# The compression's w1 tiles in the pool of 4 KB tiles instead of the weights' stage buffers

## The chip, the cores and the metric

The kernel runs on one core of a Trainium2 chip. The metric is the device time of one execution in microseconds (us). The kernel before takes 1110.68 us, the median of three runs (1110.3 to 1111.24).

## What is computed

Two layers of a decoder trunk on 512 tokens of width 1024, all in float32. Each layer normalises x, projects it once into the inputs of four token mixers, runs the mixers, and merges them under gates:

```
h = rmsnorm(x, norm_g[l])
c = split_columns(h @ w_in[l])
y_a = dilated_window_attention(...) * silu(c["a_gate"])
y_b = mla_attention(...) * silu(c["b_gate"])
y_c = nsa_attention(...) * silu(c["c_gate"])
y_d = stick_breaking_attention(...) * silu(c["d_gate"])
for i, y in enumerate((y_a, y_b, y_c, y_d)):
    gate = sigmoid(h @ w_merge[l, i] + b_merge[l, i])
    merged = merged + gate * (y @ w_branch[l, i])
x = x + merged @ w_out[l]
```

Branch C first compresses its keys and values: overlapping blocks of 32 tokens (31 of them), each flattened to 2048 numbers, go through a small network, once for keys and once for values:

```
blocks = tok[:, idx] + pos_emb
hid = gelu(blocks.reshape(B, n_cmp, NSA_CMP_BLOCK * Dk) @ w1 + b1)
return hid @ w2 + b2
```

Here w1 is 2048 x 128 for keys and again for values: four tiles of 1024 x 128 (512 KB each) per layer.

## The kernel before

Every projection is done by TensorE (PE) in float32r with three passes: a weight tile is loaded by SyncE's DMA queue (SP) into a stage buffer, then split into a high and a low part (w5 tiles) by ACT and DVE (L175 and L176, five of eight or ten k-slices) and by POOL (L100 and L185, the rest); `proj_T` then issues 24 matmuls of 128x512 (L189, L190, L191 in turn) into a PSUM accumulator pd. There are 3 stage buffers, 4 w5 tiles, 3 pd accumulators, 2 score banks pss, and 11 buffers in the pool of 4 KB tiles (per partition) called s4, which holds q, k, v, gates and the merge's accumulators. A tile takes any buffer that is free; a load or a write into it waits until the former tile's last reader is done. A merge chunk is a projection of w_merge (24 matmuls) followed by six matmuls with the branch's result y.

The program is written in one sequence, but a scheduler orders the instructions of each engine by priority and by its own idea of when operands are ready; each engine then works strictly in that order. The scores (`qk_unit`, L290) of branch A go through DVE (minimum, L300), ACT (exp, L302), DVE (L303) and POOL (L305), are transposed on PE (L325), copied by ACT (L327) and multiplied with v (L331). Branch D, stick breaking, runs in pairs of heads: scores, mask (L738), min (L740), exp (L741), ln after a table load (L744), max (L746), a running sum (L751), a subtraction (L752), exp (L753), then transposes and L331. Both are interleaved with projections of other branches, which fill PE while the other engines work.

`compress` stands in the program behind the first merge chunks. It projects the columns c_kc and c_vc (pd_1978 in layer 0), adds the positions (L609), projects c_ks and c_kw (pd_2023), and multiplies by w1 (L629, 32 matmuls of 32x128 into pd_2068): each w1 tile was loaded (L626) into a stage buffer and is used as it comes, without a split. The accumulator is copied by ACT (L632), summed over four groups by PE (L635), and the small network follows on DVE (L636 to L657).

Of the kernel before, what the change touches and what calls it, by code (L numbers as in the profile page):

```python
# [16 lines left out]
P = 128  # L17
# [69 lines left out]
def hybrid_trunk(ctx: ExitStack, tc: tile.TileContext, x, norm_g, w_in, mla_q_norm, mla_w_uq, mla_kv_norm,  # L87
# [16 lines left out]
    def mk(pool, shape, dt, tag, bufs):  # L104
        n_names[0] += 1
        return pool.tile(list(shape), dt, tag=tag, name=f"{tag}_{n_names[0]}", bufs=bufs)

    def s4(shape, dt=F32):
        return mk(sb, shape, dt, "s4", N_S4)
# [22 lines left out]
    def stage(shape):  # L132
        return mk(wp, shape, F32, "stage", 3)
# [309 lines left out]
    for l in range(DEPTH):  # L443
# [140 lines left out]
        def compress():  # L584
# [37 lines left out]
            acc = ps_d()  # L622
            for s_ in range(2):
                for hf in range(2):
                    w1 = stage([P, 8, P])
                    nc.sync.dma_start(w1, nsa_w1[l, s_, 1024 * hf:1024 * hf + 1024].rearrange("(q p) c -> p q c", p=P))  # L626
                    for q in range(8 * hf, 8 * hf + 8):
                        g = 32 * (q % 4)
                        T.matmul(acc[g:g + 32, s_ * P:(s_ + 1) * P], blocks[s_][:, q], w1[:, q % 8], start=q < 4,  # L629
                                 stop=q >= 12, skip_group_check=True)  # L630
# [76 lines left out]
        merge_chunks(l, ((0, 1),), y, am, mT)  # L707
        gd = gate_chunks("d_gate")
        ks, kw, kc, vbd = compress()
        merge_chunks(l, ((1, 0),), y, am, mT)  # L710
        c_q = [q_chunk("c_q", c, cscale[:, c:c + 1]) for c in range(2)]
# [177 lines left out]
```

## Time and profile before

| | |
|---|---|
| Median of three runs | 1110.68 us |
| The profiled execution | 1114.14 us |
| Its span | 1112.4 us |
| PE matmul busy | 1078.8 us, 97% |
| PE weight loads busy | 861.7 us |
| DVE, ACT, POOL busy | 541.5, 441.2, 464.4 us |
| HBM read | 95.67 MB, 90 GB/s over the span with what is written |

The span is the time from the first to the last instruction of the profiled execution; its own time is 1.7 us longer. The ends of matmuls are modelled, so busy time of PE is an upper bound of its work; the distance between the starts of two matmuls tells more.

### The profile page before, as it was taken

Reading aid. Unit: us, or ns where it says so; the run is one execution under the profiler, and the core shown is the slowest. Engines: PE = TensorE matmul, PEld = TensorE weight load, DVE = VectorE, ACT = ScalarE, POOL = GpSimd, SP = SyncE. Lnnn points to the kernel's source line nnn. Section 1 sums busy time; section 2 is a strip of 40 time slices with the busy share of each in tenths; the row PEclk is TensorE's granted clock in tenths of the full one; section 3 lists DMA queues with packets and bytes.
Section 4 is the critical chain, followed back from the end, with each engine's and each line's share of the span. In section 5 each row is a group of like instructions: output and inputs, shape, how many; then the busy total and the mean of one; then the engine's idle time right before and its main releaser. Section 6 shows DMA issues by size and latency. Waiting matters only on the chain.

```text
span 1112.4 us, 15422 instructions
## 1 busy us (share of the span) xinstructions
PE 1078.8 (97%) x5652; PEld 861.7 (77%) x5652; DVE 541.5 (49%) x1008; ACT 441.2 (40%) x894; POOL 464.4 (42%) x506
## 2 busy tenths in 40 slices
PE   8999999979999999999999999999799999999997
PEld 5888787758678878787888887777577787878876
DVE  6435444485835344234453546445955544532342
ACT  5424444344434434223243344435453343432232
POOL 5243354333436466452011544324334464656421
PEclk9999999989999999999999999999899999999999
DMA  7422232522232221435413322225223222233322
GB/s 245 103 57 76 76 105 58 162 66 72 71 91 75 71 73 48 133 93 153 121 57 96 95 74 70 76 77 166 62 71 94 72 71 72 72 92 90 117 77 76
DMA packets 161677, 100.87 MB, mean 91 GB/s; under 512 B 14913, under 2 KB 151489, under 8 KB 161602
## 3 DMA queue, kind: packets, MB, share of 16 engines
q1 hardware_dynamic: 160880, 98.75, 30.9%
q10 hardware_dynamic: 722, 1.14, 0.3%
q8 instruction: 45, 0.74, 0.3%
q14 instruction: 30, 0.25, 0.1%
HBM read 95.67 MB, written 4.19 MB: 90 GB/s over the span
## 4 chain that ended last, share of the span: by engine, by line
PE 83%; DVE 7%; DMA 4%; ACT 2%; issue 2%; POOL 1%; SPq 0%; POOLq 0%; DVEq 0%; ACTq 0%
PE pd L191 22%; PE pd L189 22%; PE pd L190 22%; PE po L331 5%; PE pss L290 5%; PE pt L325 4%; DMA stage<-in_w_out_dram 4%; DVE x L751 2%; DVE w L176 1%; ACT y L175 1%; DVE x L746 1%; DMA x<-in_x_dram 1%; PE pd L629 0%; PE pt L678 0%; DVE x L752 0%
## 5 line engine op out<-in xcount | busy, mean ns | idle before, releaser
L191 PE MATMUL pd<-hT,w 128*128 128x512 f32 x832 | 333.2, 401 | 11.2 <-DVE w L176 11.2
L189 PE MATMUL pd<-hT,w 128*128 128x512 f32 x832 | 335.0, 403 | 7.8 <-ACT w L175 4.7
L190 PE MATMUL pd<-hT,w 128*128 128x512 f32 x832 | 334.2, 402 | 0.0
L100 POOL TENSOR_SCALAR w<-stage 128x640 fp32r<-128x640 f32 (+1 forms) x104 | 78.1, 751 | 297.8 <-PE pd L190 192.3
L191 PEld LDWEIGHTS pd<-hT,w 128*128 128x128 f32 x832 | 157.8, 190 | 48.4 <-DVE w L176 13.6
L189 PEld LDWEIGHTS pd<-hT,w 128*128 128x128 f32 x832 | 157.8, 190 | 44.5 <-ACT w L175 6.2
L176 DVE TENSOR_TENSOR w<-stage,w 128x640 fp32r<-128x640 f32 (+2 forms) x116 | 157.5, 1357 | 69.7 <-ACT w L175 57.1
L190 PEld LDWEIGHTS pd<-hT,w 128*128 128x128 f32 x832 | 157.8, 190 | 33.6 <-issue 0.7
L185 POOL TENSOR_TENSOR w<-stage,w 128x640 fp32r<-128x640 f32 (+1 forms) x104 | 161.7, 1555 | 49.7 <-PE pd L190 39.8
L175 ACT ACTIVATE w<-stage 128x640 fp32r<-128x640 f32 (+2 forms) x116 | 87.5, 759 | 105.9 <-PE pd L190 65.8
L302 ACT ACTIVATE su<-su,stat 128x128 f32<-128x128 f32 (+3 forms) x128 | 71.2, 557 | 76.4 <-DVE stat L300 75.9
L395 POOL TENSOR_TENSOR s<-s,th 128x512 f32<-128x512 f32 x48 | 77.9, 1623 | 31.7 <-DVE th L394 31.7
L327 ACT ACTIVATE pt<-pt 128x384 f32<-128x384 f32 (+2 forms) x120 | 57.6, 521 | 77.3 <-PE pt L325 77.1
L394 DVE SCALAR_TENSOR_TENSOR th<-th,pd 128x512 f32<-128x512 f32 x48 | 32.9, 686 | 110.5 <-PE pd L191 95.2
L387 ACT ACTIVATE th<-pd,bmT 128x512 f32<-128x512 f32 x64 | 43.9, 685 | 74.6 <-PE pd L191 74.5
L305 POOL TENSOR_SCALAR su<-su,stat 128x128 f32<-128x128 f32 (+3 forms) x64 | 36.7, 579 | 79.2 <-DVE stat L303 78.1
L325 PE MATMUL pt<-small,su 128*128 128x128 f32 x336 | 60.4, 280 | 0.0
L307 POOL TENSOR_SCALAR su<-su,stat,cg 128x128 f32<-128x128 f32 (+3 forms) x64 | 41.0, 647 | 43.1 <-DVE stat L303 42.9
L189 PE MATMUL pd<-y,w 128*128 128x512 f32 x128 | 51.0, 401 | 1.9 <-ACT th L387 1.7
L325 PEld LDWEIGHTS pt<-small,su 128*128 128x128 f32 x336 | 40.2, 140 | 15.6 <-issue 8.5
L191 PE MATMUL pd<-y,w 128*128 128x512 f32 x128 | 50.5, 394 | 0.0
L190 PE MATMUL pd<-y,w 128*128 128x512 f32 x128 | 50.5, 394 | 0.0
(239 smaller groups left out, 1582.5 us busy)
## 6 DMA issues: line engine op xcount, KB each, us to landing
stage<-in_w_merge_dram SPq DMA_DIRECT2D x64, 512.0 KB, 3.9
stage<-in_w_in_dram SPq DMA_DIRECT2D x38, 512.0 KB, 3.9
stage<-in_w_branch_dram SPq DMA_DIRECT2D x64, 128.0 KB, 3.8
stage<-in_w_out_dram SPq DMA_DIRECT2D x16, 512.0 KB, 3.9
stage<-in_w_in_dram SPq DMA_DIRECT2D x20, 256.0 KB, 3.2
stage<-in_nsa_w_dram SPq DMA_DIRECT2D x8, 512.0 KB, 4.0
stage<-in_w_in_dram SPq DMA_DIRECT2D x8, 352.0 KB, 4.6
x<-in_tab_a_dram SPq DMA_DIRECT2D x4, 512.0 KB, 4.2
```

Of the source, the lines that this page charges most:

```text
L100: G.tensor_scalar(o, i, 1.0, 1.0, op0=OP.mult, op1=OP.mult)
L175: A.activation(hi, src, AF.Copy)
L176: V.tensor_tensor(lo, src, hi.bitcast(F32), op=OP.subtract)
L185: G.tensor_tensor(lo[:, a:], src[:, a:], hi[:, a:].bitcast(F32), op=OP.subtract)
L189: T.matmul(acc, sh, mh, start=start, stop=False)
L190: T.matmul(acc, sh, ml, start=False, stop=False)
L191: T.matmul(acc, sl, mh, start=False, stop=stop)
L290: T.matmul(s[:, :width], q[:, qt * P:(qt + 1) * P], k[:, :width], start=i == 0, stop=i == len(passes) - 1)
L302: A.activation(e[:, :width], e[:, :width], AF.Exp, scale=-1.0, bias=st[:, 0:1], accum_out=st[:, 1:2])
L325: T.transpose(pt[:, i], u[0][h][:, kb * P:(kb + 1) * P], ident)
L327: ready = A.activation(pT[:, :n], pt[:, :n], AF.Copy)
L395: G.tensor_tensor(acc[:, j], acc[:, j], th, op=OP.add)
```

## The change

One call in `compress` takes its tile from the pool s4 instead of stage. The shape, the load and the matmuls stay. The pools keep their sizes (11 buffers in s4, 3 in stage).

```
             for s_ in range(2):
                 for hf in range(2):
-                    w1 = stage([P, 8, P])
+                    w1 = s4([P, 8, P])
                     nc.sync.dma_start(w1, nsa_w1[l, s_, 1024 * hf:1024 * hf + 1024].rearrange("(q p) c -> p q c", p=P))
```

The scheduler answers with another order on every engine from this point to some way into branch D; the same happens in layer 1. Three places of layer 0 show it. The names carry the numbers of the tiles; s_420 to s_423 (stage_2069 to stage_2099 before) are the four w1 tiles.

On PE, right after the projection of c_ks and c_kw (pd_2023), before the change: the w1 matmuls lie between the transposes (pt) and scores (pss) of branch A.

```order
L629 MATMUL pd_2068<-stage_2069,s_410_2011 32x128 x8
L629 MATMUL pd_2068<-stage_2079,s_410_2011 32x128
L325 MATMUL pt_1706<-small,su_1673 128x128
L629 MATMUL pd_2068<-stage_2079,s_410_2011 32x128
L325 MATMUL pt_1712<-small,su_1682 128x128
L629 MATMUL pd_2068<-stage_2079,s_410_2011 32x128 x2
L290 MATMUL pss_1724<-y_297_1524,y_292_1486 128x384 x2
L290 MATMUL pss_1733<-y_298_1528,y_292_1486 128x384 x2
```

And with the change, at the end of the stretch of branch A and of D's scores of pair 0 (s_152, s_157, s_158) that now follows pd_2023 directly: the w1 matmuls come behind the first two scores of D's pair 1, and the projection of merge chunk (1, 0), pd_2147, begins only after them.

```order
L290 MATMUL pss_2693<-s_168_937,s_163_899 128x512 x2
L290 MATMUL pss_2697<-s_169_941,s_163_899 128x512 x2
L629 MATMUL pd_2068<-s_420_2069,s_410_2011 32x128 x8
L189 MATMUL pd_2147<-hT_75,w_434_2141 128x512
L190 MATMUL pd_2147<-hT_76,w_434_2141 128x512
L191 MATMUL pd_2147<-hT_75,w_435_2142 128x512
```

Before, pd_2147 and the next chunk's pd_2191 lay between these scores; now all of D's scores of pair 0 come ahead of both.

On SP, the order of the loads from the compression on, before the change:

```order
L626 DMA stage_2069<-in_nsa_w_dram 128x8x128
L626 DMA stage_2079<-in_nsa_w_dram 128x8x128
L626 DMA stage_2089<-in_nsa_w_dram 128x8x128
L626 DMA stage_2099<-in_nsa_w_dram 128x8x128
L238 DMA stage_2138<-in_w_merge_dram 128x8x128
L238 DMA stage_2138<-in_w_branch_dram 128x2x128
L238 DMA stage_2182<-in_w_merge_dram 128x8x128
L238 DMA stage_2182<-in_w_branch_dram 128x2x128
L238 DMA stage_2227<-in_w_in_dram 128x8x128
```

And now, after stage_2138, stage_2182, stage_2227 and stage_2265:

```order
L238 DMA stage_2305<-in_w_merge_dram 128x8x128
L238 DMA stage_2305<-in_w_branch_dram 128x2x128
L626 DMA s_420_2069<-in_nsa_w_dram 128x8x128
L626 DMA s_421_2079<-in_nsa_w_dram 128x8x128
L626 DMA s_422_2089<-in_nsa_w_dram 128x8x128
L626 DMA s_423_2099<-in_nsa_w_dram 128x8x128
L829 DMA s_863_4487<-in_x_dram 128x512
```

The four w1 loads moved behind five weight tiles.

On DVE, in the stick-breaking chain of pair 0 (x_493 to x_497, su_2562, su_2565), before the change: the weight split w_448, which the projection pd_2226 needs, stands inside the chain.

```order
L746 TENSOR_TENSOR su_2565<-su_2562,su_2565 128x512
L644 TENSOR_SCALAR gelu_2116<-gelu_2116 128x64
L751 SCALAR_TENSOR_TENSOR x_497_2564<-x_497_2564 128x128 x2
L751 SCALAR_TENSOR_TENSOR x_497_2564<-x_497_2564 128x384 x2
L176 TENSOR_TENSOR w_448_2230<-stage_2227,w_447_2229 128x640
L392 SCALAR_TENSOR_TENSOR s_432_2137<-th_2216,pd_2218 128x512
```

And with the change it stands behind the whole chain and the first masks of pair 1:

```order
L752 TENSOR_TENSOR x_494_2561<-x_494_2561,x_497_2564 128x1024
L738 TENSOR_TENSOR x_521_2687<-pss_2693,mask_tab 128x512
L738 TENSOR_TENSOR x_521_2687<-pss_2697,mask_tab 128x512
L752 TENSOR_TENSOR su_2562<-su_2562,su_2565 128x512
L392 SCALAR_TENSOR_TENSOR s_432_2137<-th_2172,pd_2174 128x512
L636 TENSOR_SCALAR hid_2067<-pt_2111,b_401_1966 128x32
L176 TENSOR_TENSOR w_448_2230<-stage_2227,w_447_2229 128x640
```

The chain itself is the same; its place relative to the splits is not.

## Rows read from the trace of the kernel before

**Rows 1.** The page, busy time by engine, share of the span, and instructions.

```profile
PE 1078.8 (97%) x5652; PEld 861.7 (77%) x5652; DVE 541.5 (49%) x1008; ACT 441.2 (40%) x894; POOL 464.4 (42%) x506
```

**Rows 2.** Waits of PE: total us, times, longest us.

```profile
PE pd L191 <- DVE w L176: 11.2, 4, 4.8
```

**Rows 3.** Table of stretches, layer 0: busy PE, PEld, DVE, ACT, POOL; clock; DMA share, GB/s.

```profile
235.00:240.00 5.00, 1.64 (x5) 0.59 (x4) 4.97 (x5) 3.00 (x5) 4.75 (x3) 0.85 0.00 0
240.00:245.00 5.00, 1.40 (x3) 1.16 (x4) 5.00 (x10) 0.00 (x0) 0.00 (x0) 0.50 0.02 5
```

**Rows 4.** The same table, layer 1.

```profile
780.00:785.00 5.00, 2.01 (x7) 0.78 (x5) 4.97 (x5) 3.50 (x6) 4.83 (x4) 0.96 0.00 0
785.00:790.00 5.00, 0.88 (x2) 0.79 (x3) 5.00 (x9) 0.00 (x0) 0.35 (x1) 0.50 0.00 0
```

**Rows 5.** Timeline of PE, 237 to 250: start, us, instruction, idle before and releaser.

```profile
237.46 0.50 PE L189 MATMUL pd<-hT,w 128*128 128x512 f32 x1 [2.33 <-ACT w L175]
...
243.60 0.80 PE L191 MATMUL pd<-hT,w 128*128 128x512 f32 x1 [4.62 <-DVE w L176]
...
248.83 0.39 PE L191 MATMUL pd<-hT,w 128*128 128x512 f32 x1
249.06 0.40 PE L189 MATMUL pd<-hT,w 128*128 128x512 f32 x1
```

**Rows 6.** Timeline of DVE, 233 to 250.

```profile
233.06 2.67 DVE L746 TENSOR_TENSOR x<-x,x 128x1024 f32<-128x1024 f32 x2 [2.03 <-ACT x L744]
...
242.75 0.79 DVE L176 TENSOR_TENSOR w<-stage,w 128x640 fp32r<-128x640 f32 x1
...
244.80 1.21 DVE L752 TENSOR_TENSOR x<-x,x 128x1024 f32<-128x1024 f32 x1
...
249.57 0.68 DVE L752 TENSOR_TENSOR su<-su,su 128x512 f32<-128x512 f32 x1
```

**Rows 7.** Timeline of ACT, 230 to 234.

```profile
231.97 2.01 ACT L744 ACTIVATE x<-x 128x1024 f32<-128x1024 f32 x2
```

**Rows 8.** Timeline of SP, issues of loads, 177 to 210.

```profile
179.56 26.89 SPq L626 DMA_DIRECT2D stage<-in_nsa_w_dram  x4
208.74 0.37 SPq L238 DMA_DIRECT2D stage<-in_w_merge_dram  x1
```

**Rows 9.** Timeline of POOL, 213 to 217.

```profile
213.19 0.72 POOL L100 TENSOR_SCALAR w<-stage 128x640 fp32r<-128x640 f32 x1 [2.34 <-DMA stage<-in_w_branch_dram]
...
215.12 1.57 POOL L185 TENSOR_TENSOR w<-stage,w 128x640 fp32r<-128x640 f32 x1
```

**Rows 10.** Timeline of PE, 205 to 215.

```profile
205.38 0.84 PE L629 MATMUL pd<-stage,s 128*32 128x128 f32 x18
...
207.35 0.97 PE L290 MATMUL pss<-y,y 128*128 128x384 f32 x4
208.25 0.65 PE L629 MATMUL pd<-stage,s 128*32 128x128 f32 x16
...
212.43 0.88 PE L331 MATMUL po<-pt,s 128*64 128x128 f32 x12
213.23 0.55 PE L325 MATMUL pt<-small,su 128*128 128x128 f32 x3
213.53 1.17 PE L290 MATMUL pss<-s,s 128*128 128x512 f32 x4
214.54 0.40 PE L189 MATMUL pd<-hT,w 128*128 128x512 f32 x1
```

**Rows 11.** Timeline of DVE, ACT and POOL, 208 to 210.

```profile
208.01 0.56 DVE L300 CUSTOM_DVE_ANT_0 su<-pss,x 128x384 f32<-128x384 f32 x1 [1.81 <-PE pss L290]
...
208.67 0.61 ACT L302 ACTIVATE su<-su,stat 128x384 f32<-128x384 f32 x1 [2.67 <-DVE stat L300]
...
209.66 1.18 POOL L305 TENSOR_SCALAR su<-su,stat 128x384 f32<-128x384 f32 x2 [2.90 <-DVE stat L303]
```

**Rows 12.** The w1 loads (L626), from issue to landing.

```profile
DMA to landing us min/median/max: 3.9/4.0/4.1
```

More of the change, by code (lines that the diff above doesn't have):

```diff
@@ L624, in compress @@
                 for hf in range(2):
-                    w1 = stage([P, 8, P])
+                    w1 = s4([P, 8, P])
                     nc.sync.dma_start(w1, nsa_w1[l, s_, 1024 * hf:1024 * hf + 1024].rearrange("(q p) c -> p q c", p=P))
```

## Prediction

> **What bounds the kernel now.** I read the page first. PE is busy for 1078.8 of the 1112.4 us span [rows 1], so all that a new order can win is 33.6 us of PE idleness, plus whatever time PE loses at its lower clock. The list of what PE waited for comes next. Its largest entry is the DVE half of a weight split (L176): 11.2 us in four waits, the longest 4.8 us [rows 2]. The table of short stretches shows where they sit: in layer 0 PE is busy 1.64 and 1.40 us of 235 to 240 and 240 to 245 [rows 3], and in layer 1 2.01 and 0.88 us of 780 to 785 and 785 to 790 [rows 4]. So each layer has one hole, and it lies behind the compression.
>
> The PE timeline measures the hole. The first matmul of pd_2226 starts at 237.46 after 2.33 us of idleness, the third at 243.60 after 4.62 us [rows 5]. The granted clock fell to 0.50 inside the hole, the lower level [rows 3], and the 13 matmuls from 243.60 to 248.83 take 5.23 us where at the full clock's spacing, 0.23 (248.83 to 249.06), they would take 3.0 [rows 5]. The hole therefore costs 2.33 + 4.62 + 2.2 = 9.2 us, and about 0.4 more for idleness that the modelled matmul ends cover: 9.6. In layer 1 the idleness is the same to 0.15 us, so I take 9.7 for the mean.
>
> The reason is on DVE. From 233.06 to 242.75 it works through the stick-breaking chain of head pair 0 (L746, L751), and w_448, for which PE waits, stands behind the chain: 242.75 [rows 6]. ACT's exponentials that feed the chain start only at 231.97 [rows 7]. When the hole comes PE has run out of projections: it has already done pd_2147 and pd_2191 as filler between the scores.
>
> **The change, part by part.** The same four loads and 32 small matmuls (L629, two records each) per layer remain; nothing is added or removed. What moves:
>
> *The stage ring.* Before, the w1 tiles held stage buffers from 179.56 on, and the merge weights stage_2138 were issued at 208.74 [rows 8]. Now stage_2138 and stage_2182 take the places of the first w1 loads, over 20 us earlier, so their splits move on ACT, DVE and POOL from 213 to 219 up to about 199 and 206 (when pd_1978 and pd_2023 let their weight tiles go). This hides under projections, except on POOL: the two halves of w_440 and w_441, 0.72 and 1.57 us in rows of their kind [rows 9], now stand ahead of the normalisation of su_1700.
>
> *The w1 loads.* The tile addresses of the built program show that the first one takes the buffer of a D key tile of pair 0, which the score matmul pss_2594 reads last; the second that of the A values, the third that of A's gate, the fourth that of the first. So on SP they now wait for PE, and what stands behind them (x rows, stage_2350) waits too; x is needed only at the layer's end, and stage_2350 cannot start before w_448 is split anyway, so I price that at nothing. If it were uncovered it would be one load, 4.0 us [rows 12]. On ACT the copy of the compression's sums (L632) now waits for the last L629, and the tanh of chunk (1, 0), L753 and the split w_447 are queued behind it; in the walk below w_447 is there at 233.6, before PE wants it, so this costs nothing; with 4 us more it would be on the path.
>
> *PE's order.* L629 and pd_2147 move behind A's last softmax pair and D's scores, which therefore run from 205.4 without filler.
>
> Now the walk on layer 0's clock. The block from pd_2023's end to pss_2697 has 12 score matmuls 512 wide, 8 of 384, 4 of 256, 4 of 128, 20 transposes and 20 PV matmuls (L331, two records each). At the spacings of [rows 10] (1.01 for four of 512, 0.90 for four of 384, 0.80 for six PV matmuls, 0.10 to 0.17 for a transpose, and an estimated 1.0 for the eight narrow ones) that is 3.0 + 1.8 + 1.0 + 2.7 + 2.0 to 3.4 = 10.5 to 11.9; I take 11.3, so PE alone would be done at 216.7. But a score takes 0.66 us to DVE's minimum, another 0.66 to ACT, 0.99 to POOL and 0.59 there [rows 11], with two score banks in all. Put in each engine's new order: su_1700 is normalised at 208.8 (POOL had to split w_440 and w_441 first), and PE waits 0.8 us for it; the scores then go at the pace at which DVE empties the two banks: pss_2566 at 209.2 (behind the minimum of su_1763), pss_2574 at 211.9, pss_2578 at 212.6; A's last transposes follow su_1772's normalisation, 214.0 to 214.5; the four narrow scores go from 214.5 to 215.6, the last PV of A to 216.7. pss_2693 then waits for L738 of pss_2590, which DVE has queued behind L339, which waits for that PV: 217.9, and pss_2697 ends at 218.9. The first w1 load starts at 215.9 and lands 4.0 us later [rows 12]: 219.9. So L629 starts at 220.0, and PE has lost 220.0 - 216.7 = 3.3 us; I add 0.6 for handovers that I took at their shortest: 3.9.
>
> From there PE has no wait in the walk. 30 matmuls of merge chunk (1, 0) at 0.233 (7.0), L629 (2.5), 30 of the next chunk (7.0), L635 (0.4), two 384-wide scores (0.9) and two matmuls of pd_2226 bring it to 238.3. DVE's chain: exponentials at 221.1 (behind ACT's work for A, D's first exponentials and a table load), then 1.09 us to L746 as in [rows 6, 7], then 9.1 us of the same L746 and L751 (9.7 from 233.06 to 242.75, less 0.6 for L392), 5.3 of L752, L751 and L738 as from 244.80 to 250.2 [rows 6], 1.6 of L392, L636 and L176: w_448 is there at 238.2. A dead heat. If DVE's half-load is 1 us dearer, PE waits 1 us.
>
> One gain beside it: between 205.38 and 214.54 the 32 matmuls, cut into seven pieces, cost what is left of 9.16 us after 0.90 + 2 x 1.0 + 0.80 + 12 transposes (1.2 to 2.0), that is 3.5 to 4.3 us; in pieces of eight they cost 0.65 each [rows 10], 2.6. I take 0.9.
>
> Sum per layer: 9.7 + 0.9 - 3.9 = 6.7 us, 13.4 for both. The profiled execution took 1114.14 us, of which 1112.4 are the span, 0.3% above the median of the runs; the gain is an absolute one, so 1110.7 - 13.4 = 1097.3. Bounds: with no lost time at all in the block the gain is 2 x 10.6, 1089.5; with the walk 3 us later in each layer, 1103.3.
>
> **The rivals.** *The softmax chain starves PE.* Four A scores and ten D scores now run bare. If each handover costs 0.2 us more, the block ends 3 to 4 us later, DVE's chain with it, and the gain shrinks to some 3 us a layer: 1104. For it: the walk is tight everywhere, and POOL and DVE now split weights inside it. Against it: the hops are measured, not assumed.
>
> *The clock falls in the block.* Behind the hole of before, largely at the lower level, 13 matmuls took 5.23 us instead of 3.0 [rows 5]; at that ratio the block of 11.3 us would take 8.4 more. With lost time of 3.9 + 8.4 = 12.3 against the 10.6 won, each layer is 1.7 us longer: 1114. It decides from the point where more than 6.7 us a layer go that way. Against it: in the hole of before the clock fell only with PE nearly still for several us [rows 3], and here PE works over three quarters of the time. The Trainium skill (TensorE: Matmul & The Clock Gate, "A second HAM failure mode: psum-queue depth-cycling") speaks for it: small idle gaps between groups that cycle through PSUM banks can keep the clock going back and forth. No row here shows that with gaps this short.
>
> *The gain is handed back.* DVE's second chain (pair 1) and the C branch follow. If they, not PE, set the pace to 320, what PE wins is waited for there: within 2 us of before, 1109 to 1111. Against it: DVE's chain of pair 0 also ends 12 us sooner.
>
> **How the numbers follow.** Forecast 0.69 (1090 to 1101), starved softmax 0.14 (1101 to 1107), clock 0.07, handed back 0.06, better than the forecast 0.04. A measurement of this kernel can tell about 0.2%, 2.2 us. Faster 0.87, same 0.06, slower 0.07. Leaving out the clock, the handing back and the best cases, the range is 1090 to 1105.
>
> **What would show it.** Right: the hole at 235 to 245 and the one at 780 to 790 are gone, with no clock below 0.9 there; L629 starts near 220 and PE waits there for a w1 load, 1 to 2 us; the largest wait of PE is no longer L176. Wrong: a granted clock of 0.5 between 205 and 225, L629 later than 224, or new waits of PE on L176 beyond 240.

## The result and the profile after

The changed kernel takes 1098.09 us (median of four runs, 1096.96 to 1098.76) against 1110.49 us on the same chip (median of four runs there too): a ratio of 0.9887, 95% interval 0.9870 to 0.9904, 12.4 us faster. 1097.3 was forecast. In a later set of runs, beside the last experiments, it took 1098.6 against 1111.21: 0.9883 (0.9868 to 0.9898). The profiled execution took 1098.76 us, its span 1096.7; all rows of this section are from it.

The page's line of busy times, and the waits of PE (total, times, longest), which answer to [rows 1] and [rows 2]:

```profile
PE 1071.2 (98%) x5652; PEld 859.2 (78%) x5652; DVE 541.8 (49%) x1008; ACT 440.0 (40%) x894; POOL 459.2 (42%) x506
...
PE pss L290 <- DVE su L738: 2.7, 2, 1.5
PE pt L325 <- POOL su L305: 2.7, 4, 1.2
PE pd L189 <- DVE s L568: 2.4, 2, 1.2
PE pd L191 <- DVE w L176: 1.8, 2, 0.9
PE pd L629 <- DMA s<-in_nsa_w_dram: 1.7, 2, 0.9
```

The instructions are the same 5652, but PE's wait for L176 fell from 11.2 us in four waits to 1.8 in two. A wait for the w1 load is new. (A wait of 2.5 us before and 2.9 now, for in_norm_g at the start of the program, is left out here.) The table of stretches, columns as in [rows 3], with the two holes of [rows 3, 4] and the block before the first:

```profile
215.00:220.00 5.00, 2.62 (x24) 1.72 (x22) 4.23 (x8) 3.40 (x6) 2.78 (x4) 0.98 0.52 144
220.00:225.00 5.00, 4.90 (x29) 3.75 (x30) 2.62 (x3) 3.80 (x4) 0.39 (x1) 0.68 1.07 305
235.00:240.00 5.00, 5.00 (x25) 4.22 (x24) 4.81 (x11) 2.42 (x4) 1.23 (x2) 1.00 0.20 51
240.00:245.00 5.00, 5.00 (x25) 4.10 (x25) 2.50 (x9) 0.26 (x1) 0.35 (x2) 1.00 0.83 238
780.00:785.00 5.00, 5.00 (x27) 4.19 (x26) 2.52 (x3) 1.31 (x2) 2.28 (x2) 1.00 0.39 113
785.00:790.00 5.00, 5.00 (x27) 4.14 (x26) 3.24 (x8) 2.13 (x4) 1.47 (x2) 1.00 0.43 108
```

Both holes are full, at a granted clock of 1.00. The price stands at 215 to 225: PE is idle for 2.38 us, and then works for some us at the lower of its two clock levels, so that the mean of 220 to 225 is 0.68. PE's timeline (start, us, instruction, idle before and releaser) shows why, and where it meets w_448:

```profile
217.97 1.19 PE L290 MATMUL pss<-s,s 128*128 128x512 f32 x4 [1.55 <-DVE su L738]
220.10 1.08 PE L629 MATMUL pd<-s,s 128*32 128x128 f32 x16 [0.94 <-DMA s<-in_nsa_w_dram]
221.11 0.80 PE L189 MATMUL pd<-hT,w 128*128 128x512 f32 x1
...
223.32 0.39 PE L191 MATMUL pd<-hT,w 128*128 128x512 f32 x1
...
239.36 0.40 PE L191 MATMUL pd<-hT,w 128*128 128x512 f32 x1
```

L629 stands behind the scores of D's first pair and two of its second, waits 0.94 us for its load, and the first matmuls behind it run 0.80 and 0.63 us long instead of 0.40. The first matmul by w_448's DVE half starts at 239.36 without a wait. DVE wrote that half, in the step behind its chain [rows 6], a little earlier:

```profile
236.97 0.81 DVE L176 TENSOR_TENSOR w<-stage,w 128x640 fp32r<-128x640 f32 x1
```

It ends at 237.78; before, it ended at 243.54 [rows 6]. SP's issues answer to [rows 8]:

```profile
178.92 0.37 SPq L238 DMA_DIRECT2D stage<-in_w_merge_dram  x1
...
215.44 2.43 SPq L626 DMA_DIRECT2D s<-in_nsa_w_dram  x2
```

The merge weight that was issued at 208.74 now leaves at 178.92, and the first w1 load, no longer in the stage buffers, at 215.44. From issue to landing the w1 loads take

```profile
DMA to landing us min/median/max: 4.6/4.8/6.4
```

where they took 4.0 [rows 12].

### The profile page after: what moved, and what is told of

Same layout as the page of the kernel before. It is cut to its first block, busy times and chain, and to the rows that moved or that the text cites. A ratio compares the mean times of both kernels' runs of the same rounds, so it can differ in the third digit from the quotient of the medians.

```text
span 1096.7 us, 15435 instructions
## 1 busy us (share of the span) xinstructions
PE 1071.2 (98%) x5652; PEld 859.2 (78%) x5652; DVE 541.8 (49%) x1008; ACT 440.0 (40%) x894; POOL 459.2 (42%) x506
## 3 DMA queue, kind: packets, MB, share of 16 engines
q10 hardware_dynamic: 722, 1.14, 0.3%
## 4 chain that ended last, share of the span: by engine, by line
PE 86%; DMA 5%; DVE 4%; issue 2%; ACT 1%; POOL 1%; SPq 0%; POOLq 0%; DVEq 0%; ACTq 0%
PE pd L189 23%; PE pd L191 23%; PE pd L190 23%; PE po L331 5%; PE pss L290 5%; PE pt L325 4%; DMA stage<-in_w_out_dram 4%; DVE x L751 1%; DMA s<-in_nsa_w_dram 1%; ACT y L175 1%; DVE w L176 1%; POOL w L185 1%; DMA x<-in_x_dram 0%; PE pt L678 0%; DVE x L752 0%
## 5 line engine op out<-in xcount | busy, mean ns | idle before, releaser
L100 POOL TENSOR_SCALAR w<-stage 128x640 fp32r<-128x640 f32 (+1 forms) x104 | 74.4, 715 | 313.4 <-PE pd L190 192.8
L176 DVE TENSOR_TENSOR w<-stage,w 128x640 fp32r<-128x640 f32 (+2 forms) x116 | 160.2, 1381 | 71.2 <-ACT w L175 58.5
L185 POOL TENSOR_TENSOR w<-stage,w 128x640 fp32r<-128x640 f32 (+1 forms) x104 | 158.1, 1521 | 49.3 <-PE pd L190 39.2
```

What stands on the lines that cost most here:

```text
L100: G.tensor_scalar(o, i, 1.0, 1.0, op0=OP.mult, op1=OP.mult)
L176: V.tensor_tensor(lo, src, hi.bitcast(F32), op=OP.subtract)
L185: G.tensor_tensor(lo[:, a:], src[:, a:], hi[:, a:].bitcast(F32), op=OP.subtract)
```

## A common account for all runs

Two things changed at once: PE's order (L629 and the projections pd_2147 and pd_2191 stand behind D's first scores), and the stage buffers (the merge weights come 30 us earlier). To compare runs I add up, over stretches of 5 us, 5.00 less PE's busy time multiplied by its granted clock. For 220 to 225 above that is 5.00 - 4.90 x 0.68 = 1.7 us lost. Two places per layer matter: the **first place** (200 to 250, and 740 to 800 in layer 1) holds the bare block (A's last and D's first scores, without projections between them) and the hole behind D's first pair; the **second place** (250 to 320, 800 to 865) holds DVE's chain of D's second pair. The first number is layer 0, the second layer 1.

| Run | L629 and projections | stage buffers | first place | second place | median us | ratio to before (95%) |
|---|---|---|---|---|---|---|
| before | early | held by w1 | 9.8, 10.2 | 2.6, 2.1 | 1110.49 | 1 |
| after | late | free | 5.6, 3.5 | 2.1, 2.1 | 1098.09 | 0.9887 (0.9870 to 0.9904) |
| e15_after_again | late | free | 3.8, 3.6 | 2.1, 2.6 | 1098.6 | 0.9883 (0.9868 to 0.9898) |
| e1_layer0 | late, early | free, held | 3.8, 9.1 | 2.6, 2.6 | 1105.24 | 0.9942 (0.9930 to 0.9954) |
| e3_s2 | early | free | 10.5, 10.4 | 2.6, 2.4 | 1114.13 | 1.0025 (1.0015 to 1.0035) |
| e5_no_w1 | early | free | 9.7, 10.6 | 2.6, 2.6 | 1110.93 | 0.9991 (0.9983 to 1.0000) |
| e4_stage_late | late | held | 14.6, 15.4 | 4.9, 3.9 | 1125.41 | 1.0116 (1.0099 to 1.0134) |
| e9_s2_late | late | free | 5.1, 4.7 | 5.8, 5.8 | 1110.94 | 0.9993 (0.9984 to 1.0001) |
| e8_half | in part | 1 of 4 held | 5.7, 7.6 | 5.3, 6.5 | 1110.25 | 0.9988 (0.9979 to 0.9998) |
| e6b_dma_late | late | free | 8.4, 8.0 | 7.6, 7.4 | 1114.4 | 1.0022 (1.0013 to 1.0031) |
| e10_first_s2 | late | free | 3.6, 3.2 | 2.6, 2.1 | 1099.03 | 0.9887 (0.9869 to 0.9905) |
| e14_split_load | late | free | 3.4, 3.8 | 2.6, 2.6 | 1098.03 | 0.9889 (0.9870 to 0.9908) |
| e13_split_late | late | free | 5.4, 5.0 | 5.7, 6.2 | 1105.43 | 0.9945 (0.9932 to 0.9957) |

The account is rough: the four numbers of a row, less those of e15_after_again (12.1), come within 4 us of the difference of the times, by the ratios. For before it is 24.7 - 12.1 = 12.6. Over the whole span the same sum is 39.4 us before and 27.1 us after, so nearly all of the gain lies in these two places (24.7 against 13.3). The spans of these two executions differ by more, 15.7 us, since the profiled execution of the kernel before took 1114.14 us, 3.6 more than the median.

## The experiments

**e1_layer0: the change in layer 0 alone.**

```diff
-                    w1 = s4([P, 8, P])
+                    w1 = (s4 if l == 0 else stage)([P, 8, P])
```

> The w1 tiles take key buffers in layer 0 and stage buffers in layer 1. Both theories: half of the gain, 1104.3 us (1110.5 less 6.2), if each layer's gain is its own and nothing of it comes from the seam between the layers. The stretch 235 to 245 of layer 0 is full as in the changed kernel, and layer 1 keeps the idle stretch of the kernel before. Over 1107 or under 1101.5 would mean that one layer bears nearly all.

1105.24 us against 1111.9 on the same chip: about half the gain. Its table of stretches has both patterns in one execution:

```profile
235.00:240.00 5.00, 4.82 (x23) 3.56 (x22) 4.97 (x11) 2.90 (x4) 1.69 (x2) 1.00 0.01 4
240.00:245.00 5.00, 5.00 (x25) 4.11 (x24) 2.56 (x10) 0.61 (x2) 0.54 (x2) 1.00 1.01 275
...
775.00:780.00 5.00, 1.36 (x4) 0.59 (x4) 5.00 (x8) 0.90 (x2) 2.64 (x2) 0.81 0.00 0
780.00:785.00 5.00, 3.52 (x9) 2.81 (x9) 5.00 (x7) 1.06 (x1) 0.00 (x0) 0.51 0.47 133
```

The gain is each layer's own.

**e3_s2: the stage buffers free, but the old order.** The w1 tiles become eight half tiles in the pool of 2 KB tiles, which has room early.

```diff
-                    w1 = s4([P, 8, P])
-                    nc.sync.dma_start(w1, nsa_w1[l, s_, 1024 * hf:1024 * hf + 1024].rearrange("(q p) c -> p q c", p=P))
+                    w1 = [s2([P, 4, P]) for _ in range(2)]
+                    for i in range(2):
+                        r0 = 1024 * hf + 512 * i
+                        nc.sync.dma_start(w1[i], nsa_w1[l, s_, r0:r0 + 512].rearrange("(q p) c -> p q c", p=P))
...
```

> The w1 tiles are eight half tiles from the pool of 2 KB tiles: out of the stage buffers, and without a wait for a key buffer. TensorE's order is then that of the kernel before (L629 early, the projections pd_2147 and pd_2191 ahead of D's first scores), and the stage buffers are as free as in the changed kernel. Order theory (mine: the gain comes from the projections that stand behind D's first scores): the idle stretch at 235 to 245 stays, 1107 to 1111 us. Buffer theory (rival: the gain comes from the stage buffers that w1 no longer blocks, so that the merge weights are ready earlier): 1096 to 1100 us.

1114.13 us: no gain. SP's issues show the merge weight as early as in the changed kernel:

```profile
178.94 0.37 SPq L238 DMA_DIRECT2D stage<-in_w_merge_dram  x1
```

And yet the hole is there, as in [rows 3]:

```profile
235.00:240.00 5.00, 0.74 (x2) 0.30 (x2) 4.97 (x7) 1.38 (x3) 3.98 (x3) 0.88 0.02 0
240.00:245.00 5.00, 2.33 (x5) 1.45 (x6) 5.00 (x8) 1.06 (x1) 0.00 (x0) 0.50 0.01 2
```

Early weights alone bring nothing: the buffer theory falls. Why it is 0.25% slower than before, with the two places hardly different, I did not settle.

**e5_no_w1: the same question without any w1.**

```diff
-                    w1 = s4([P, 8, P])
-                    nc.sync.dma_start(w1, nsa_w1[l, s_, 1024 * hf:1024 * hf + 1024].rearrange("(q p) c -> p q c", p=P))
...
-                        T.matmul(acc[g:g + 32, s_ * P:(s_ + 1) * P], blocks[s_][:, q], w1[:, q % 8], start=q < 4,
+                        T.matmul(acc[g:g + 32, s_ * P:(s_ + 1) * P], blocks[s_][:, q], hT[0].bitcast(F32)[:, q % 8, :P], start=q < 4,
```

> Leaves out w1: its loads are gone and L629 multiplies by a slice of the layer's input instead, so no buffer of any pool is taken and no load is waited for. Order theory: L629 is early and the projections are spent ahead of D's scores, the idle stretch at 235 to 245 stays, 1106 to 1111 us. Buffer theory: the gain of the changed kernel and the wait of 0.9 us per layer for w1 besides, 1095 to 1098 us.

1110.93 us, first place 9.7 and 10.6. With the loads gone altogether, the hole stays as long as the projections are spent ahead of D's scores. So neither the w1 loads nor their buffers cost the time.

**e4_stage_late: the new order, the stage buffers still held.** On the kernel before (w1_first holds the first L629; after() adds a dependence of its second argument on its first):

```diff
...
-                        V.tensor_tensor(part(0, qt, h), s[:, :w], mask_tab[:, S + 1 - w:], op=OP.subtract)
+                        masked = V.tensor_tensor(part(0, qt, h), s[:, :w], mask_tab[:, S + 1 - w:], op=OP.subtract)
+                if pr == 0:
+                    after(masked, w1_first[0], "w1 late")
```

> The kernel before, w1 in the stage buffers, with one dependence added: the first L629 waits for the last masked score of D's first pair. TensorE's order around the block is then near that of the changed kernel, while the stage buffers are blocked for longer than before. Order theory: the idle stretch at 235 to 245 goes, and the merge weights come late instead, TensorE waiting some 3 to 5 us per layer for them: 1099 to 1107 us. Buffer theory: no gain, and the longer block costs: 1111 to 1120 us.

1125.41 us, far above what I gave for the order alone (1099 to 1107), and above the range of the buffer theory too (1111 to 1120). SP's issues say why:

```profile
178.91 39.91 SPq L626 DMA_DIRECT2D stage<-in_nsa_w_dram  x4
218.93 0.52 SPq L238 DMA_DIRECT2D stage<-in_w_merge_dram  x1
```

The four w1 loads stretch over 40 us, because the later L629 now holds the stage buffers, and the merge weights leave only at 218.93. The projections that ought to fill PE behind D's scores have no weights. So the order alone fell too: e3 and e4 together say that both are needed, late projections **and** their weights in time.

**e9_s2_late: order and free stage buffers, without a key buffer.** (A key buffer is one of the pool s4 that held a key or value tile, as the w1 tiles of the changed kernel take it.) The tiles of e3_s2 and the dependence of e4_stage_late:

```diff
...
+                    w1 = [s2([P, 4, P]) for _ in range(2)]
...
+                    after(masked, w1_first[0], "w1 late")
```

> The half tiles of the run e3_s2, loaded early into the 2 KB pool, and the dependence of the run e4_stage_late: the first L631 waits for the last masked score of D's first pair. TensorE's order around the block is that of the changed kernel, the stage buffers are free of w1, no key buffer is involved and no w1 load is waited for. If the gain needs only late projections with their weights ready (order and free stage buffers together): the idle stretch at 235 to 245 is gone, and the time is that of the changed kernel less its wait of 0.9 us per layer and some of its low clock: 1094 to 1098 us. If the key buffer does something else that brings the gain: 1104 to 1113 us.

1110.94 us, a clear miss. But the first place is nearly as good as in the changed kernel, 5.1 and 4.7:

```profile
235.00:240.00 5.00, 3.80 (x15) 2.79 (x16) 4.20 (x8) 2.18 (x4) 1.53 (x2) 1.00 0.51 146
240.00:245.00 5.00, 5.00 (x31) 3.92 (x31) 1.25 (x3) 0.39 (x1) 0.00 (x0) 1.00 0.76 222
295.00:300.00 5.00, 3.85 (x17) 2.79 (x15) 5.00 (x7) 0.69 (x1) 2.27 (x3) 1.00 0.00 0
300.00:305.00 5.00, 1.51 (x4) 1.22 (x5) 5.00 (x5) 0.39 (x1) 1.91 (x1) 0.85 0.05 15
```

The old hole is mostly closed and a new one stands 60 us later, in D's second pair. The timelines of DVE and PE there (L758 is the scan, L751 in the other kernels):

```profile
297.49 5.23 DVE L758 TENSOR_TENSOR_SCAN x<-x 128x128 f32<-128x128 f32 x4
302.64 0.79 DVE L176 TENSOR_TENSOR w<-stage,w 128x640 fp32r<-128x640 f32 x1
...
303.49 0.79 PE L191 MATMUL pd<-hT,w 128*128 128x512 f32 x1 [4.65 <-DVE w L176]
```

DVE has four scans ahead of a weight split, and PE waits 4.65 us for the split. In the changed kernel a split stands ahead of the scans, and the projection that it feeds runs beside them:

```profile
283.47 1.33 DVE L176 TENSOR_TENSOR w<-stage,w 128x640 fp32r<-128x640 f32 x1
284.73 3.80 DVE L751 TENSOR_TENSOR_SCAN x<-x 128x128 f32<-128x128 f32 x4
288.45 0.65 DVE L568 SCALAR_TENSOR_TENSOR s<-th,pd 128x512 f32<-128x512 f32 x1
...
284.86 0.50 PE L191 MATMUL pd<-hT,w 128*128 128x512 f32 x1 [0.88 <-DVE w L176]
```

The kernel before has the same order there:

```profile
290.30 1.34 DVE L176 TENSOR_TENSOR w<-stage,w 128x640 fp32r<-128x640 f32 x1
291.56 3.79 DVE L751 TENSOR_TENSOR_SCAN x<-x 128x128 f32<-128x128 f32 x4
```

My theory knew only the first place. The next two runs lost time at the same second place.

**e8_half: one w1 tile back to the stage buffers.**

```diff
-                    w1 = s4([P, 8, P])
+                    w1 = (stage if s_ == 0 and hf == 0 else s4)([P, 8, P])
```

> Only the first of the four w1 tiles goes back to a stage buffer; the others keep their key buffers. L629 of the first tile is early, pd_2147 is spent between A's scores, and 20 matmuls of pd_2191 and 24 of L629 stand behind D's first scores. Order theory, in parts: A's bare stretch (4.2 us of idle time per layer) is filled, but the cover behind D's first scores is shorter by 28 matmuls or 6.5 us, so 2 to 5 us of the idle stretch return at 235 to 245, with low clock: 1097 to 1105 us. Buffer theory: one tile in four in the stage buffers, 1098 to 1101 us with the idle stretch gone.

1110.25 us, above both ranges. The first place loses 5.7 and 7.6 us; 3.8 and 5.6 of them lie from 235 and from 785 on, where the order theory gave 2 to 5. The second place loses 5.3 and 6.5, which I had not counted. DVE has a split ahead of the scans here, and yet PE runs out of matmuls beside them and waits for the gate's L568 behind them, 8.4 us in two waits:

```profile
291.85 0.81 DVE L176 TENSOR_TENSOR w<-stage,w 128x640 fp32r<-128x640 f32 x1
292.59 4.19 DVE L751 TENSOR_TENSOR_SCAN x<-x 128x128 f32<-128x128 f32 x4
...
297.41 0.80 PE L189 MATMUL pd<-hT,w 128*128 128x512 f32 x1 [4.20 <-DVE s L568]
```

**e6b_dma_late: the first w1 load later.** It waits for L339:

```diff
+                    if s_ == 0 and hf == 0:
+                        after(a_done, ld, "w1 behind A")
...
-                finish_pair(acc, ga, y[0], pr)
+                a_done = finish_pair(acc, ga, y[0], pr)
```

> The changed kernel with the first w1 load held until A's last block is normalised on VectorE (L339, which ends at 217.6 in layer 0; the load now leaves at 215.4). L629 is still the first matmul behind D's first scores and comes 2.2 us later. If the landing of w1 sets the end of the bare block as the prediction has it: 2.2 us more per layer, 1102.5 us; with a longer low clock behind it up to 1105. If the wait for w1 is hidden by DVE's chain (which sets when the merge weights are split): 1098 us, no change.

1114.4 us where I gave 1102.5. PE's timeline has L629 (L631 here) 1.7 us later than in the changed kernel:

```profile
221.77 1.08 PE L631 MATMUL pd<-s,s 128*32 128x128 f32 x16 [2.62 <-DMA s<-in_nsa_w_dram]
```

The first place loses 8.4 and 8.0 us, with the clock at 0.61 and 0.71 from 220 to 230. The second place loses 7.6 and 7.4: DVE has the split behind the scans here too (scans from 288.12, split at 291.80), and PE waits 5.7 us for it. This run therefore doesn't price the landing of w1 by itself.

**e6c_swap: compress() coded behind the next merge chunk.**

```diff
-        ks, kw, kc, vbd = compress()
         merge_chunks(l, ((1, 0),), y, am, mT)
+        ks, kw, kc, vbd = compress()
```

> The changed kernel with the compression coded behind the first merge chunk instead of ahead of it: the w1 tiles ask for their key buffers later, and L629 stands in the middle of pd_2226, behind the scores of D's second pair. Order theory: the projections are spent ahead of D's second scores again, but the D scores come bunched; if pd_2226 still meets its split weight w_448 without an idle stretch, 1095 to 1099 us and the wait for w1 is hidden; if not, 1100 to 1108 us. It tells whether the wait for w1 and the bare block can be had back.

1129.93 us, ratio 1.0168 (1.0152 to 1.0183); outside both cases given. The key buffers come free later still, the w1 loads leave at 244.89, and PE waits 6.5 us per layer for them. The first place loses 16.6 and 13.3 us, the second 3.0 and 4.9; by the ratios some 6 us more lie elsewhere, which I did not trace. The later order has to have its loads in time as well.

**e13_split_late: the second place alone.** The changed kernel, with the split of w_481 held until the scans are done; all that comes earlier keeps its order. (lows lists the DVE halves of the splits, n_low is their number ahead of this merge chunk.)

```diff
...
+                    if pr == 1 and j == 1:
+                        after(scan, lows[n_low], "split behind the scans")
```

> The changed kernel, all four w1 tiles in key buffers, with one dependence added in D's second pair: the split of merge weight w_481 on VectorE waits for the scans behind which it stands in e9_s2_late and e6b_dma_late. All orders up to there are the changed kernel's. Two-place theory: first place as in the changed kernel (3.5 to 5.6 us lost per layer), second place 7 to 10 us instead of 2.1, as TensorE waits for w_481 behind 4 scans and more (5 to 8 us later than at 284.8): 1107 to 1114 us, so that this one order takes the whole gain back. If the second place does not decide: 1098 to 1101 us.

1105.43 us: 6.8 more than the changed kernel beside it, about half the gain. I had given 1107 to 1114. The second place is 5.7 and 6.2 instead of 2.1 and 2.6. The first place is 5.4 and 5.0 instead of 3.8 and 3.6: in this execution the clock fell there in both layers, in layer 0 so:

```profile
220.00:225.00 5.00, 5.00 (x24) 3.81 (x17) 3.31 (x3) 3.12 (x4) 0.00 (x0) 0.76 0.94 277
```

So the account has 7.2 us more at the second place and 3.0 more at the first, for 6.8 us more time; by that, between 3.8 and 6.8 us are the second place's. DVE and PE there:

```profile
282.68 4.27 DVE L753 TENSOR_TENSOR_SCAN x<-x 128x128 f32<-128x128 f32 x4
286.86 0.66 DVE L569 SCALAR_TENSOR_TENSOR s<-th,pd 128x512 f32<-128x512 f32 x1
...
287.67 0.76 PE L190 MATMUL pd<-y,w 128*128 128x512 f32 x1 [4.50 <-DVE s L569]
291.74 0.50 PE L192 MATMUL pd<-hT,w 128*128 128x512 f32 x1 [0.20 <-DVE w L177]
```

Lines count one higher here: L569 is the gate's L568, L177 the split L176. PE waits 4.50 us for the gate behind the scans and only 0.20 for the split. In the changed kernel the projection by w_481 (reading hT, from 284.86) covered the scans; here it stands behind them, at 291.74, and a product that reads y had to go ahead of it. The wait is at the place where I put it, but for the gate and not for the split, and it is smaller than I gave. PE's waits there are 9.2 us in the two layers together, against 4.2 in the profiled execution of the changed kernel (L568 2.4, L176 1.8).

**e10_first_s2: the changed kernel without the wait for the first w1 tile.** Only the first tile goes to the 2 KB pool, loaded early, with e4's dependence:

```diff
+                    if 2 * s_ + hf < 1:
+                        w1 = [s2([P, 4, P]) for _ in range(2)]
+                    else:
+                        w1_ = s4([P, 8, P])
+                        w1 = [w1_[:, :4], w1_[:, 4:]]
...
```

DVE has the split ahead of the scans, as in the changed kernel.

> The changed kernel, with only the first w1 tile as two half tiles in the 2 KB pool, loaded early, and the dependence of e4_stage_late, so that the first matmul by w1 stays behind D's first scores. The other three tiles keep their key buffers. VectorE's order in D's second pair is that of the changed kernel (the split of the merge weight stands between the scans), unlike in e9_s2_late. Two-place theory (the gain is what the late projections bring at the first place, 200 to 250, if the second place, 250 to 320, keeps its 2.1 us): first place 3.5 to 4.5 us lost per layer, second place 2.1, and 1095 to 1098 us. If the key buffer of the first tile matters beyond its order: 1102 to 1111 us.

1099.03 us, 1 us above the range of the two-place theory. First place 3.6 and 3.2, second 2.6 and 2.1, both close to what I gave; DVE's split stands at 282.69, the four scans from 283.95 on. The gain of the changed kernel is there without a key buffer for the first tile. But it is not faster. L629 (L635 here) follows the scores at once, and PE meets a new wait at w_448, 0.50 us in layer 0 and 0.49 in layer 1:

```profile
219.42 0.65 PE L635 MATMUL pd<-s,s 128*32 128x128 f32 x16
...
238.48 0.50 PE L191 MATMUL pd<-hT,w 128*128 128x512 f32 x1 [0.50 <-DVE w L176]
```

**e14_split_load: each w1 load in two halves.**

```diff
+                    for i in range(2):
+                        r0 = 1024 * hf + 512 * i
+                        nc.sync.dma_start(w1[:, 4 * i:4 * i + 4], nsa_w1[l, s_, r0:r0 + 512].rearrange("(q p) c -> p q c", p=P))
```

> The changed kernel with each w1 load issued as two loads of half a tile, so that the first four matmuls of L629 need only the first half. Landing theory (the end of the bare block is set by the landing of w1): the first half lands some 0.5 to 1 us earlier, 1095 to 1098 us. If the landing time is that of a load's start and not of its size: no change, 1098 to 1100 us.

1098.03 us against 1098.6 of e15_after_again: no difference, first place 3.4 and 3.8. The first half does land in time: L629 (L631 here) follows the scores at 218.94 without a wait. But SP issues eight loads instead of four, from 215.27 to 225.56, and PE now waits for the last half tile, 0.29 us in layer 0 and 1.14 in layer 1:

```profile
228.61 0.43 PE L631 MATMUL pd<-s,s 128*32 128x128 f32 x8 [0.29 <-DMA s<-in_nsa_w_dram]
...
767.11 0.43 PE L631 MATMUL pd<-s,s 128*32 128x128 f32 x8 [1.14 <-DMA s<-in_nsa_w_dram]
```

The waits for w1 are 1.4 us in both runs. This run moved them, and does not tell what the landing costs.

**e15_after_again: the changed kernel once more, with no edit.**

> The changed kernel again, beside the three above on the same chip: 1098 to 1100 us, with the low clock at 220 to 225 in one layer, both or none. It tells the spread of the first place between executions.

1098.6 us. This execution lost no clock at 220 to 225, and waited 0.48 us for w1 there instead of 0.94, so that the first place is 3.8 us where the earlier execution lost 5.6:

```profile
220.00:225.00 5.00, 4.92 (x35) 3.91 (x36) 2.53 (x3) 4.21 (x5) 0.82 (x1) 1.00 1.15 296
```

No run beat the changed kernel by more than can be measured.

## Why the prediction was right, point by point

**The hole of 9.7 us per layer goes: right, and its cause is shown.** The account finds 9.8 and 10.2 us at the first place of before. (The prediction counts 13 matmuls from 243.60 to 248.83; PE's timeline has 12, so the low clock cost 2.4 us there and not 2.2.) The hole goes where late projections find their weights ready (after, e9, e10), and stays or grows where one of the two is missing (e3 and e5: weights early, projections spent; e4: projections late, weights too). So neither of what the walk calls "the stage ring" and "PE's order" is enough alone. The prediction counted only costs of the earlier merge weights and did not say that the gain hangs on weights in time. In e4 they leave 10 us later than before the change; whether late projections with weights at the time of before, 208.74, would have gained, no run shows.

**The bare block loses 3.9 us: right in size.** The first place loses 3.5 to 5.6 us per layer afterwards, 3.5 to 3.8 where the clock held. Some terms inside were off. The block began 0.7 us earlier than in the walk and L629 still started at 220.10: that is 4.7 us behind the issue of its load, not 4.0, and PE's wait for POOL was 1.2, not 0.8. PE waits 0.94 and 0.80 us for w1, just under the 1 to 2 given as a sign. The clock's fall, 1.7 us in one layer of one execution, was not in the sum.

**The dead heat at w_448: right, and it matters more than I saw.** DVE's half was written at 237.78 (walk: 238.2), PE wanted it at 239.36 in that execution. In e10, without a wait for w1, PE was there at 237.98 and had to wait until 238.48. So most of the wait for w1, which I counted as lost, could not have been won: e10 takes away 0.48 and 0.87 us of it (as in e15) and waits 0.50 and 0.49 at w_448 instead.

**L629 in large pieces, 0.9 us per layer: near in size, not tested.** PE's busy time fell by 7.6 us [rows 1], at equal instructions. The low clock behind the two holes was 2.4 and 2.7 of it (12 and 13 matmuls in 5.23 and 5.71 us, at 0.233 each otherwise), and 1.7 came back at 220 to 225, so 4.2 are left. That has room for my 1.8. In PE's timelines of layer 0 the seven pieces of before take 3.29 us from their starts to the next one's, the two of now 1.01 + 1.44 = 2.45, the first of them partly at the lower clock: 0.84 us less, near my 0.9. What the pieces cost the matmuls beside them is not in it, and no run changes this alone.

**The rival of a gain handed back, 0.06: it did not happen here, but my reason against it was not the one that held.** I argued that DVE's first chain ends sooner. What decides is whether PE, at D's second pair, has a projection to do beside DVE's four scans. In the changed kernel, as in the one before, a weight's split stands ahead of them and gives it one. e13 shows the price of turning them round, with the order of PE that follows: 3.8 to 6.8 us. e9 and e6b had them turned and lost the whole gain, with other changes beside it. e8 had the split ahead and still ran out of projections at the gate, so the split alone is not enough. Why the scheduler turns the order in e9 and e6b and not in e10, no run shows. So the forecast rested on an order 60 us behind the change that the prediction didn't read; that it stayed as it was is luck as far as the prediction goes. The range held the time, but the chance for this rival was low for what the runs show.

**The clock in the block, 0.07: it falls, but for less.** I priced it at 8.4 us a layer. In one layer of the profiled execution the granted clock was 0.68 in the mean of 220 to 225, at the lower level until some 223.3, behind a stretch with PE busy for 2.62 of 5 us (idle times of at most 1.55 us), and it cost 1.7. In e6b and e13 it fell in both layers. The Trainium skill (TensorE: Matmul & The Clock Gate, "A second HAM failure mode: psum-queue depth-cycling") says that short idle gaps between groups cycling through PSUM banks can make the clock go back and forth. The traces agree in part: in each layer where the clock fell there was one fall and one recovery, in some executions, and no going back and forth.

## What to carry to other kernels

A buffer pool is also an order: a tile that must wait for a buffer keeps its consumers behind other work, and the matmuls held back with it can fill a later hole. That pays only if their weights are there, so the two effects have to be tested together and apart. And when one order changes, read the next place where the same engines meet: here it was whether TensorE had a projection to do beside four scans of VectorE, 60 us later, that let the gain stand.

## What I had not expected of the hardware

- The same program lost its clock behind the block in one execution (a mean of 0.68 from 220 to 225) and not in another (1.00). PE had been busy for 2.62 of the 5 us before in the first and for 2.96 in the second, where it waited 0.48 us for w1 instead of 0.94; in e6b, with 2.60 before and 3.23 in the next 5 us, the clock stood at 0.61 and 0.71 for 10 us.
- The w1 loads took 4.8 us from issue to landing where they took 4.0 before [rows 12], with the same bytes in other buffers and at another time. The four issues were spread over 26.89 us before [rows 8] and stand within 6.2 us now; whether that is the reason, no run shows.
